# Placing side work in a one-core decoder step: value products, weight sums, load order, memory splits, convolution

## The chip, the cores and the metric

The kernel runs on one core of one Trainium2 chip. The metric is device time in microseconds of one execution. Before the change it is 1868.93 us, the median of 3 runs (1867.21 to 1870.87). The profile is of one execution.

The core has engines that run side by side, each with its own instruction queue: TensorE (PE, with its weight loads PEld), VectorE (DVE), ScalarE (ACT), GpSimd (POOL) and SyncE (SP), which here issues nearly all DMA transfers. An engine takes its instructions in the order in which the program was written out for it, and one that waits holds up all behind it.

## What is computed

One step of a one-layer hybrid decoder on 1024 prompt tokens and 8 x 4 sample tokens. Cut to what matters here:

```python
u, v, cq, ckv, kpe = split_in(rms_norm(xp, g_mix[l]) @ w_in[l])
a_out, _ = chunk_gmlp(u, v, w_s[l], b_s[l], ln_v_g[l], ln_v_b[l])
q = mla_queries(cq, pos_p, g_q_a[l], w_uq[l], g_qk_q[l])
k, vv = mla_keys_values(ckv_n, kpe, pos_p, w_uk[l], w_uv[l], g_qk_k[l])
b_out = mla_prompt_attend(q, k, vv)
xp = xp + merge_out(a_out, b_out, g_out_a[l], g_out_b[l], w_o[l])
mk, mv = mem_kv(mem_prompt, g_mem_in[l], w_mk[l], w_mv[l], g_mk[l])
xp = xp + mem_attend(rms_norm(xp, g_mem_x[l]), mk, mv, w_mq[l], g_mq[l], w_mo[l])
y, buf = conv_ffn(rms_norm(xp, g_ffn[l]), ..., w_up[l], w_conv[l], b_conv[l], w_down[l])
```

The sample tokens go through the same layer; their latent attention (`mla_sample_attend`) reads 8 x 4096 cached latents by a page table.

## The kernel before

Every large product is done in three matmuls: each float32 operand is split into a rounded part and a remainder (`split`, L187: the rounded part on ACT by default, the remainder on DVE), and `mm3` (L179) adds high x high, high x low and low x high. That is why almost all of PE's time stands under L185.

Tiles come from pools with a fixed number of buffers; a tile waits until the one that held its buffer before has been read for the last time. Where the program opens `manual_schedule` for an engine, that engine's instructions keep the order of the program text. Elsewhere a planner that models the engines' times sets the order.

*Phase 1* (`phase1`, L289) projects all tokens. For each half `hf` of the gated part it projects v (`proj`, L375), normalises it into `vgh`/`vgl` (L455 to L477), projects u (L485), and multiplies v by the gate matrices (L491 to L498). `squares` (L343) makes the inverse norms of the tokens; the engine of its root steps can be chosen. All v projections of the second half come in the next round of the loop.

*Phase 2a* (`phase2a`, L646) is the prompt's latent attention: 16 head units of 3 or 4 steps, 56 steps in all. PE, ACT, DVE and POOL follow the text. At each step `t` the loop (L763 to L794) runs the transposes, scores, exponentials and value products, and then everything listed in `extra[t]`. What stands in `extra` is set at L716 to L728: splits of the second half's weights (`split_w`), the sample tokens' projections (`tok_s`), the preparation of each head (`preps`: transposes of k and q, for head h of group 4 at steps 21 to 25), the projections of heads 4 to 7 (`late`, whose `norm` at L883 ends with the rope on POOL and with k at L906 and L907), and 26 `weight_sums` (L809). A weight sum loads 512 KB of weights on SP (L814 or L819), makes four additions on POOL (L822 to L825) and stores 512 KB on SP (L826). Its tile `wsum` has two buffers, which `split_w`'s raw weights use first. From step 32 on, `sample_prep` and `pages_ahead` (L1102) prepare the sample tokens: the latter loads the page numbers, the rope tables and the first three quads of latents.

*Phase 2b* (`phase2b`, L1119) is the sample tokens' attention: 128 pairs of page blocks, two to a quad of four pages, 16 to a request. `steps` (L1192) writes them out by hand for PE, ACT, DVE and POOL, from n = -10; SP is left to the planner. For a quad, POOL rotates the keys (`quad_rot`, L1307: `krq`), ACT and POOL or DVE split the latents (`quad_prep`, L1318: `ch`, `cl`), PE multiplies (`pair_score`, L1349), ACT squares (L1366, L1369), and PE forms the value products 20 pairs later (`quad_pv`, L1437). `quad_sums` (L1333) squares the rope keys of the second copy of the latents, `ck`. The ck pool has 15 buffers (L1132); the same buffers also serve `b4` (L1148), raw loads of phase 2a's last results, and at the end the raw weights and memory of the next stage (`raws`, L1204). At its start the text issues the load of `b4` (L1149), then inside `steps` those of `fold4` (L1201) and `wuv` (L1203).

*Behind it* come `mem_kv` (L1483: keys and values of the 256 memory tokens, with the last request's softmax and `batch_out` in between), `out_proj` (L1648), `mem_attention` (L1696) and `ffn` (L2070). In `ffn_up` (L2074) each of 11 rounds computes a `gate` block (L2115) for two halves h of the tokens, with the convolution behind it, and then two `value` blocks (L2160). `block` (L2086) makes seven products; `z` (L2098) is a DVE sum that frees one of two `X` buffers.

Of the kernel before, what the change touches and what calls it, by code (L numbers as in the profile page):

```python
# [6 lines left out]
FR = mybir.dt.float32r  # L7
I32 = mybir.dt.int32
AF = mybir.ActivationFunctionType
ALU = mybir.AluOpType  # L10
# [3 lines left out]
P = 128  # L14
# [140 lines left out]
class Net:  # L155
# [133 lines left out]
    def phase1(self):  # L289
# [140 lines left out]
        for hf in range(2):  # L430
# [8 lines left out]
            for i0, i1 in ((0, 3), (3, 6), (6, 8), (8, 9)):  # L439
                m, tn = i1 - i0, TILES[i0][1]  # L440
                if hf == 0 and i0 == 3:
                    squares(6, 8, nc.gpsimd)
# [203 lines left out]
    def phase2a(self):  # L646
# [69 lines left out]
        put(split_w, (2, 2, 3, 3))  # L716
        spread(tok_s, 0, 7)
# [9 lines left out]
        for j, x in enumerate(sums):  # L727
            extra[4 + j * 26 // 18 if j < 18 else 36 + (j - 18) * 13 // 8].append(lambda x=x: self.weight_sums(half(), *x))  # L728
# [390 lines left out]
    def phase2b(self):  # L1119
# [29 lines left out]
        nc.sync.dma_start(b4, self.b_dram)  # L1149
# [6 lines left out]
        for n in range(11):  # L1156
            at(n + 3 if n < 7 else 2 * n - 3, 0, lambda: next(mix, 0))
# [10 lines left out]
        at(last - 2, 3, lambda: self.split(*wk0, raws[0].rearrange("p (k n) -> p k n", k=8)))  # L1168
        for b in range(NB):
# [3 lines left out]
            for r, (k, pos) in enumerate(((12, 0), (13, 0), (14, 0), (14, 3), (15, 0), (16, 0), (17, 0), (17, 3), (18, 2), (19, 2), (20, 0), (20, 2), (21, 3))):  # L1173
# [8 lines left out]
                lambda b=b: self.batch_out(pt, st[b], 1, ppt),  # L1182
# [9 lines left out]
        def steps(n0, n1):  # L1192
            for n in range(n0, n1):
# [40 lines left out]
        with tc.manual_schedule(engines={E.SP}):  # L1234
# [5 lines left out]
            mem = self.mem_kv(raws, wk0)  # L1240
# [207 lines left out]
    def batch_out(self, p, s, part, pp=None):  # L1448
# [10 lines left out]
        nc.vector.tensor_scalar(oo[:, :256], oo[:, :256], rd, None, ALU.mult)  # L1459
# [23 lines left out]
    def mem_kv(self, raws, wk0):  # L1483
# [38 lines left out]
        def values(k):  # L1522
            wh, wl = (x.rearrange("p k n -> p (k n)").rearrange("p (k n) -> p k n", k=2) for x in self.stream(I["w_mv"][k // 2], 8))
            for i in range(2):
                t = slice(i * P, i * P + P)
                self.mm3(av[i], [(mh[:, k + e, t], ml[:, k + e, t]) for e in range(2)],
# [547 lines left out]
    def ffn_up(self, ops, rows, norm, first):  # L2074
# [40 lines left out]
        def gate(w, fs, h, prev):  # L2115
# [20 lines left out]
            nc.vector.tensor_tensor(G[:, :, 2:], G[:, :, 2:], row, ALU.mult)  # L2136
# [254 lines left out]
```

## Time and profile before

| | before |
|---|---|
| median of 3 runs | 1868.93 us |
| profiled execution, whole time | 1869.24 us |
| its span, first to last instruction | 1867.5 us |
| mean granted TensorE clock | 0.989 |

The page gives each engine's busy time, share of the span and number of instructions. A row of the list of waits names the waiting engine and line, the engine and line that ended the wait, and then total, count and longest wait in us. A row of the timeline gives start, duration, engine, line, operation, what it writes and reads, and in brackets the idle time ahead of it with its releaser. A row of the windows gives, for a stretch, the busy time of PE, PEld, DVE, ACT and POOL with their counts, the granted clock, and the DMA engines' busy share and GB/s. A row of DMA issues gives count, KB of one, and median us from issue to landing.

### The profile page before, as it was taken

The page shows a single profiled execution, that of the slowest core. Times are in us where ns is not written, and L with a number is a line of the kernel's source. Part 1 is how long each engine was busy: PE and PEld are TensorE (multiplying, and loading weights), DVE is VectorE, ACT ScalarE, POOL GpSimd, SP SyncE. Part 2 cuts the span into 40 slices and gives each one's busy share as a digit, 9 for nine tenths or more (in the row PEclk, how much of TensorE's full clock was granted, in tenths as well). Part 3 has the DMA queues.
Part 4 walks back from the last instruction along what each step waited for, and adds up shares of the span by engine and source line. Part 5 has one row for each costly group of instructions (what it writes and reads, how often), then busy time and mean ns, then how long its engine had stood idle before and what let it go on. Part 6 is the DMA issues. An engine that isn't in the chain of part 4 may idle for free.

```text
span 1867.5 us, 39356 instructions
## 1 busy us (share of the span) xinstructions
PE 1819.1 (97%) x14222; PEld 1713.6 (92%) x14222; DVE 1349.1 (72%) x2789; ACT 927.7 (50%) x1965; POOL 703.9 (38%) x862
## 2 busy tenths in 40 slices
PE   9999898998999999999999999999999999999999
PEld 8899776768999999998799978899999999999999
DVE  7864666665787667876645676889888898878664
ACT  7335676775555565555433456533323333344442
POOL 2011247524544444544223010267776677400000
PEclk9999899999999999999999999999999999999999
DMA  8101155547776666664554345312222222495252
GB/s 324 37 17 61 34 165 164 192 144 224 214 210 186 173 188 180 177 180 145 155 171 134 116 163 162 123 63 87 74 91 81 70 80 70 122 344 169 77 154 76
DMA packets 153187, 261.18 MB, mean 140 GB/s; under 512 B 20897, under 2 KB 97538, under 8 KB 152994
## 3 DMA queue, kind: packets, MB, share of 16 engines
q1 hardware_dynamic: 152130, 257.63, 44.7%
q8 instruction: 112, 1.84, 0.4%
q10 hardware_dynamic: 864, 1.05, 0.2%
q14 instruction: 81, 0.66, 0.1%
HBM read 212.79 MB, written 45.82 MB: 138 GB/s over the span
## 4 chain that ended last, share of the span: by engine, by line
PE 79%; issue 6%; DVE 5%; DMA 3%; SPq 3%; POOL 2%; ACT 2%; DVEq 0%; POOLq 0%; ACTq 0%
PE s L185 14%; PE d L185 12%; PE mm L185 9%; PE b L185 8%; PE X L185 7%; PE E L185 7%; PE F L185 7%; PE A L185 3%; PE y L185 2%; PE o L992 2%; PE tp L977 1%; PE tp L185 1%; SPq L1297 1%; PE o L1444 1%; DMA ck<-ck 1%
## 5 line engine op out<-in xcount | busy, mean ns | idle before, releaser
L185 PE MATMUL s<-w2h,ch 128*128 128x288 f32 (+1 forms) x1024 | 304.6, 297 | 0.0
L185 PE MATMUL s<-w2h,cl 128*128 128x288 f32 (+1 forms) x1024 | 296.9, 290 | 3.3 <-POOL cl L1329 3.3
L185 PE MATMUL s<-w2l,ch 128*128 128x288 f32 (+1 forms) x1024 | 295.6, 289 | 0.0
L185 PEld LDWEIGHTS s<-w2h,ch 128*128 128x128 f32 x1024 | 193.7, 189 | 8.3 <-issue 2.5
L185 PEld LDWEIGHTS s<-w2h,cl 128*128 128x128 f32 x1024 | 193.4, 189 | 5.5 <-POOL cl L1329 5.4
L185 PEld LDWEIGHTS s<-w2l,ch 128*128 128x128 f32 x1024 | 193.8, 189 | 0.0
L1372 DVE TENSOR_REDUCE ss<-sq 128x16 f32<-128x1024 f32 x128 | 155.3, 1213 | 32.5 <-ACT sq L1369 32.0
L1329 POOL TENSOR_TENSOR cl<-cT,ch 128x512 fp32r<-128x512 f32 x64 | 82.8, 1293 | 128.4 <-ACT ch L1325 115.9
L1369 ACT ACTIVATE sq<-s 128x512 f32<-128x512 f32 x128 | 76.5, 598 | 88.8 <-PE s L185 88.7
L1366 ACT ACTIVATE sq<-s 128x512 f32<-128x512 f32 x128 | 76.8, 600 | 74.7 <-PE s L185 74.3
L191 ACT CAST a<-brb 128x528 fp32r<-128x528 f32 x77 | 48.8, 634 | 112.5 <-PE d L185 105.8
L185 PE MATMUL d<-a,w 128*128 128x264 f32 x768 | 95.4, 284 | 1.1 <-DVE G L2168 1.1
L192 DVE TENSOR_TENSOR a<-brb,a 128x528 fp32r<-128x528 f32 x77 | 54.2, 706 | 57.6 <-ACT a L191 57.6
L185 PEld LDWEIGHTS d<-a,w 128*128 128x128 f32 x768 | 94.3, 188 | 1.3 <-issue 1.3
L2039 POOL TENSOR_TENSOR lo<-s,hi 128x1024 fp32r<-128x1024 f32 x20 | 63.1, 3154 | 45.7 <-ACT hi L2038 45.7
L185 PE MATMUL mm<-wlo,xh 128*128 128x256 f32 (+3 forms) x272 | 78.1, 289 | 0.1
L185 PE MATMUL mm<-whi,xh 128*128 128x256 f32 (+3 forms) x272 | 78.0, 288 | 0.0
L2094 ACT COPY a<-A 128x264 f32<-128x264 f32 x43 | 16.2, 376 | 124.5 <-PE A L185 116.3
L185 PE MATMUL mm<-whi,xl 128*128 128x256 f32 (+3 forms) x272 | 77.5, 289 | 0.0
L1325 ACT CAST ch<-cT 128x512 fp32r<-128x512 f32 x128 | 73.4, 626 | 2.6 <-PE tp L1005 2.6
L185 PE MATMUL d<-a,hi 128*128 128x264 f32 x552 | 72.0, 284 | 0.0
L1368 DVE TENSOR_TENSOR S<-s,S 128x64 f32<-128x64 f32 x128 | 28.0, 219 | 57.6 <-ACT sq L1366 57.3
(742 smaller groups left out, 6420.5 us busy)
## 6 DMA issues: line engine op xcount, KB each, us to landing
cT<-cT SPq DMA_DIRECT2D x256, 160.0 KB, 2.7
ck<-ck SPq DMA_DIRECT2D x256, 144.0 KB, 3.5
raw<-w_up SPq DMA_DIRECT2D x44, 512.0 KB, 3.6
wsumd<-wsum SPq DMA_DIRECT2D x26, 512.0 KB, 3.6
actd<-cv SPq DMA_DIRECT2D x44, 264.0 KB, 2.4
brb<-actd SPq DMA_DIRECT2D x44, 264.0 KB, 5.6
wsum<-w_down SPq DMA_DIRECT2D x22, 512.0 KB, 3.6
raw<-wsumd SPq DMA_DIRECT2D x20, 512.0 KB, 3.7
```

What stands on the lines that cost most here:

```text
L185: self.nc.tensor.matmul(out, l, r, start=first and i == 0, stop=last and i == len(seq) - 1)
L191: {"act": nc.scalar.copy, "pool": nc.gpsimd.tensor_copy, "dve": nc.vector.tensor_copy}[eng](hi, src)
L192: low = lambda: nc.vector.tensor_tensor(lo, src, hi, ALU.subtract)
L977: nc.tensor.transpose(tp[:, z * P : z * P + P], u[e][:, j * P : j * P + P], self.ident)
L992: nc.tensor.matmul(u["o"][g : g + 64, o : o + m * P], s["v"][:, j, h % 4], th[:, z * P : (z + m) * P], start=j == 0, stop=b == len(banks) - 1,
L1325: nc.scalar.copy(d["h"][:, k], src[k])
L1329: (nc.vector if k else nc.gpsimd).tensor_tensor(d["l"][:, k], src[k], d["h"][:, k], ALU.subtract)
L1366: nc.scalar.activation(sq[:, 0], ps[:, :, n0 : n0 + 256], AF.Square)
L1368: nc.vector.tensor_tensor(S, ps[:, :, sc : sc + 32], S, ALU.add)
L1369: nc.scalar.activation(sq[:, 1], pt.rearrange("p (e d) -> p e d", e=2), AF.Square)
L1372: yield lambda: nc.vector.tensor_reduce(s["ss"][:, g0 : g0 + 2].rearrange("p e (z h) -> p z e h", z=2), sq.rearrange("p z e (h d) -> p z e ...
L2039: eng.tensor_tensor(lo, src, hi, ALU.subtract)
```

## The change

Seven edits, in the order of the text:

1. `squares(6, 8)` makes its root steps on DVE instead of POOL; and in the first half the second half's first three v projections are written ahead of the gate products.
2. `split_w` moves from steps 2, 2, 3, 3 to 4, 5, 6, 7; `tok_s` from steps 0 to 7 to steps 4 to 11. The 26 weight sums move from steps 4 to 28 (18 of them) and 36 to 47 (8) to steps 7 to 11 (5), 25 to 31 (7) and 36 to 50 (14).
3. The loads of `b4`, `fold4` and `wuv` are each put, on SP, behind the page loads that the text has issued by then (n = 1, 16, 64). The steps of the mix that reads `b4` move from n = 3 to 15 to n = 5 to 17. `quad_sums` of the first quad moves from n = 1 to n = 4.
4. Four of the memory's eight splits move from `mem_kv` into the last steps of phase 2b, into two ck buffers.
5. The split of the first memory key weights moves from step 126 to 124.
6. The last request's normalisation runs on POOL instead of DVE.
7. `gate` becomes a generator that stops ahead of the convolution; in the first round both halves' products come first, then both convolutions. In the other rounds the order stays.

```diff
-                    squares(6, 8, nc.gpsimd)
+                    squares(6, 8)
...
+            if hf == 0:
+                ready.update({i: proj(w, i, 256) for i in range(3)})
             for g in range(4):
...
-        put(split_w, (2, 2, 3, 3))
-        spread(tok_s, 0, 7)
+        put(split_w, (4, 5, 6, 7))
+        spread(tok_s, 4, 11)
...
-        for j, x in enumerate(sums):
-            extra[4 + j * 26 // 18 if j < 18 else 36 + (j - 18) * 13 // 8].append(lambda x=x: self.weight_sums(half(), *x))
+        times = [*range(7, 12), *range(25, 32), *(36 + j * 16 // 14 for j in range(14))]
+        for t, x in zip(times, sums):
+            extra[t].append(lambda x=x: self.weight_sums(half(), *x))
...
-        nc.sync.dma_start(b4, self.b_dram)
...
-            at(n + 3 if n < 7 else 2 * n - 3, 0, lambda: next(mix, 0))
+            at((5, 6, 7, 8, 9, 10, 11, 12, 13, 15, 17)[n], 0, lambda: next(mix, 0))
...
-        at(last - 2, 3, lambda: self.split(*wk0, raws[0].rearrange("p (k n) -> p k n", k=8)))
+        at(last - 4, 3, lambda: self.split(*wk0, raws[0].rearrange("p (k n) -> p k n", k=8)))
+        mem0 = []
+
+        def mem_split(k):
+            if k % 2 == 0:
+                x = self.t(p, [P, 4, 288], FR, "ck", 15).rearrange("p k n -> p (k n)")[:, :1024].rearrange("p (k z n) -> p k z n", k=2, z=2)
+                mem0.extend((x[:, e, 0], x[:, e, 1]) for e in range(2))
+            self.split(*mem0[k], raws[1].rearrange("p (k n) -> p k n", k=4)[:, k], self.col("g_mem_in", k))
+
+        for k in range(4):
+            at(last - 3 + k, 3, mem_split, k)
...
-                if n == 16:
-                    nc.sync.dma_start(self.fold4, I["c_fold4"])
-                if n == 64:
-                    nc.sync.dma_start(wuv, I["w_uv"])
+                for k, dst, src in ((1, b4, self.b_dram), (16, self.fold4, I["c_fold4"]), (64, wuv, I["w_uv"])):
+                    if n == k:
+                        self.tc.add_manual_dep(
+                            nc.sync.dma_start(dst, src).ins, self.page_dma[-1].ins.name,
+                            mybir.DependencyInfo(mybir.DependencyClass.NoSync, mybir.DependencyReason.DATA), reason="order",
+                        )
...
-                    at(n + (6 if 0 <= Q < 2 else 3), 0, self.quad_sums, Q + 1, quads[Q + 1], st[(Q + 1) // 8])
+                    at(n + (6 if Q < 2 else 3), 0, self.quad_sums, Q + 1, quads[Q + 1], st[(Q + 1) // 8])
...
-        nc.vector.tensor_scalar(oo[:, :256], oo[:, :256], rd, None, ALU.mult)
+        if final:
+            nc.gpsimd.tensor_tensor(oo[:, :256], oo[:, :256], rd.broadcast_to([P, 256]), ALU.mult)
+        else:
+            nc.vector.tensor_scalar(oo[:, :256], oo[:, :256], rd, None, ALU.mult)
...
-        mh = self.t(p, [P, 8, 256], FR, "mh")
-        ml = self.t(p, [P, 8, 256], FR, "ml")
+        mh, ml = (self.t(p, [P, 4, 256], FR, x) for x in ("mh", "ml"))
...
-        xs = [(mh[:, k], ml[:, k]) for k in range(8)]
+        xs = mem0 + [(mh[:, k], ml[:, k]) for k in range(4)]
...
-                if h == 0:
-                    self.split(mh[:, k], ml[:, k], mr[k // 4][:, k % 4], self.col("g_mem_in", k))
+                if h == 0 and k > 3:
+                    self.split(*xs[k], mr[k // 4][:, k % 4], self.col("g_mem_in", k))
...
             nc.vector.tensor_tensor(G[:, :, 2:], G[:, :, 2:], row, ALU.mult)
+            yield G
...
-            return cv, G
+            yield cv
...
-            cvs, prev = [], None
+            cvs, prev, its = [], None, []
             for h in range(2):
-                cv, prev = gate(w, fs, h, prev)
-                cvs.append(cv)
+                it = gate(w, fs, h, prev)
+                prev = next(it)
+                its.append(it)
+                if q or h:
+                    cvs += [next(x) for x in its]
+                    its = []
```

More of the change, by code (lines that the diff above doesn't have):

```diff
@@ L1181, in phase2b @@
                 lambda b=b: self.batch_out(pt, st[b], 0),
-                lambda b=b: self.batch_out(pt, st[b], 1, ppt),
+                lambda b=b: self.batch_out(pt, st[b], 1, ppt, b == NB - 1),
                 lambda b=b: self.batch_close(pt, ppt, b, st.pop(b)),
@@ L1239, in phase2b @@
             self.wp = self.open("w", bufs=3, side="right")
-            mem = self.mem_kv(raws, wk0)
+            mem = self.mem_kv(raws, wk0, mem0)
             for f in late:
@@ L1446, in quad_pv, with batch_out @@
             )
-    def batch_out(self, p, s, part, pp=None):
+    def batch_out(self, p, s, part, pp=None, final=False):
         nc = self.nc
@@ L1481, in stream, with mem_kv @@
         return hi, lo
-    def mem_kv(self, raws, wk0):
+    def mem_kv(self, raws, wk0, mem0):
         nc, tc, I, O = self.nc, self.tc, self.I, self.O
@@ L1525, in values @@
                 t = slice(i * P, i * P + P)
-                self.mm3(av[i], [(mh[:, k + e, t], ml[:, k + e, t]) for e in range(2)],
+                self.mm3(av[i], [tuple(x[:, t] for x in xs[k + e]) for e in range(2)],
                          [(wh[:, e], wl[:, e]) for e in range(2)], first=k == 0, last=k == 6)
```

## The prediction

> **What bounds the kernel now.** I read the page first, then who TensorE (PE) waited for, then the granted clock around those waits.
>
> ```profile
> span 1867.5 us, 39356 instructions
> PE 1819.1 (97%) x14222; PEld 1713.6 (92%) x14222; DVE 1349.1 (72%) x2789; ACT 927.7 (50%) x1965; POOL 703.9 (38%) x862
> ```
>
> PE is busy 1819.1 of 1867.5 us. The change removes no matmul, so it can only win some of the 48 us in which PE stands still, and what those stops cost afterwards. The list of PE's waits (total, times, longest):
>
> ```profile
> PE tp L930 <- POOL k L907: 5.6, 2, 2.9
> PE tp L977 <- ACT pr L969: 5.2, 6, 1.3
> PE s L1344 <- ACT S L1347: 4.2, 1, 4.2
> PE mm L185 <- ACT vgh L191: 3.8, 1, 3.8
> PE m L1465 <- DVE oo L1459: 2.2, 1, 2.2
> PE X L185 <- DVE z L2098: 1.6, 1, 1.6
> PE b L185 <- DVE ml L198: 1.6, 2, 1.3
> PE b L185 <- ACT mh L195: 0.9, 1, 0.9
> ```
>
> Each edit aims at one of these rows. A stop also costs clock. Stretches just behind six of the stops, and one undisturbed stretch first (columns: busy time and count of PE, PEld, DVE, ACT, POOL, then the granted clock):
>
> ```profile
> 52.00:58.00 6.00, 6.00 (x53) 6.00 (x52) 5.92 (x27) 2.64 (x7) 0.00 (x0) 1.00 0.00 0
> 64.90:70.90 6.00, 6.00 (x24) 5.61 (x25) 4.52 (x18) 0.00 (x0) 0.00 (x0) 0.50 0.56 182
> 306.40:309.80 3.40, 3.40 (x13) 2.97 (x12) 3.02 (x8) 2.29 (x4) 3.16 (x5) 0.51 0.32 110
> 319.30:323.50 4.20, 4.20 (x20) 3.30 (x21) 0.00 (x0) 1.55 (x4) 3.89 (x6) 0.60 0.37 126
> 437.70:443.00 5.30, 5.30 (x23) 5.30 (x24) 3.52 (x5) 3.08 (x7) 3.03 (x4) 0.50 0.80 183
> 927.70:931.10 3.40, 3.40 (x13) 3.40 (x14) 2.02 (x5) 1.26 (x4) 0.00 (x0) 0.50 0.54 138
> 1207.60:1211.00 3.40, 3.40 (x18) 3.40 (x17) 3.37 (x4) 0.00 (x0) 3.40 (x2) 0.50 0.00 0
> ```
>
> PE counts as busy there but runs at half clock: 24 matmuls in 6 us against 53. A stop costs its idle time plus (1 - clock) times the slow stretch: 3.0, 1.7, 1.7, 2.7, 1.7 and 1.7 us in the order of the rows.
>
> The Trainium skill ("TensorE: Matmul & The Clock Gate", section "HAM oscillation — how this bites in real kernels") asks only that PE's gaps stay under about 3.4 us. The trace disagrees: half clock follows gaps of 2.2 and 1.6 us as well. By the page those two stops would cost 3.4 us less, and my sum would be smaller by that.
>
> **Part by part.** Times below are of the profiled execution.
>
> *Value products ahead of the gate's (L491), squares on DVE (L442).* PE stands 3.8 us before the first gate product, waiting for vgh. The change puts three projections of the next weight half there, 3 x 24 matmuls at 6.00/53 = 0.113 us, 8.1 us of work that is done later today anyway. They need only the split of v1; this cover is over twice the stall. If the cover failed the stall would stay as it is. Idle 3.8 + clock 3.0 = **-6.8 us**. Moving the small roots from POOL to DVE takes about 11 tiny instructions to DVE, where PE does not wait: 0.
>
> *Weight sums, splits and sample latents in phase 2a (L716 to L728).*
>
> ```profile
> 231.94 0.44 PE L977 MATMUL tp<-ident,pr 128*128 128x128 f32 x2 [1.31 <-ACT pr L969]
> 305.09 1.04 POOL L907 TENSOR_TENSOR k<-kr,hr 128x512 f32<-128x512 f32 x1
> 313.40 0.74 POOL L607 TENSOR_TENSOR rp<-q,tq_c 128x256 f32<-128x256 f32 x1
> 318.18 1.05 POOL L907 TENSOR_TENSOR k<-kr,hr 128x512 f32<-128x512 f32 x1
> 311.22 0.49 DVE L894 TENSOR_TENSOR rq<-hr,sq_tok 128x16 f32<-128x16 f32 x1
> L822 POOL TENSOR_TENSOR wsum<-wsum 128x256 f32<-128x256 f32 x13 | 9.5, 728 | 23.4 <-DMA wsum<-w_down 23.4
> 391.05 0.74 POOL L825 TENSOR_TENSOR wsum<-wsum 128x256 f32<-128x256 f32 x1
> 417.57 0.13 POOL L1269 MEMSET S<- 128x32 f32 x1 [25.78 <-PE tp L977]
> 419.89 0.46 POOL L1314 TENSOR_TENSOR krq<-cT,cosT 128x128 f32<-128x128 f32 x1 [2.19 <-PE o L992]
> 422.62 0.46 PE L1344 MATMUL s<-bd,krq 128*128 128x128 f32 x2 [0.23 <-DVE b_last L1009]
> wsum<-w_down SPq DMA_DIRECT2D x7, 512.0 KB, 3.5
> wsumd<-wsum SPq DMA_DIRECT2D x7, 512.0 KB, 3.3
> SPq L814 <- DMA wsumd<-wsum: 73.6, 22, 4.7
> ```
>
> Today POOL's rope for heads 4 to 7 stands behind weight sums, and PE waits for k twice (5.6 us idle, 3.4 us clock). With no sums in steps 12 to 24 both go but for about 1 us: -8. The splits and latents leave ACT's path in steps 0 to 3, where waits for pr lie (the 1.3 us at 231.9 is the longest of the six); I take -3, that one and its slow clock of 1.7 (bounds 0 and -5.2, all six). So PE would reach the end of phase 2a about 11 us earlier.
>
> But POOL runs in program order, and phase 2b opens with POOL's krq, for which its first PE instruction waits. The sums have two buffers, and each load waits for the store before it (the wait of L814). One buffer's round is load 3.5, four subtractions of 0.73 with their gaps 3.2, store 3.3: 10.0 us, so 5.0 us a sum at best. Measured, the 13 sums between 319.2 and 391.8 took 72.6/13 = 5.6 us each. Before, POOL is then free for 25.8 us. After, only five sums are done before step 25 and 21 come behind it. They can start when the second k is done: its input at 311.2, less 4.5 (first stall and its clock) and 3, plus 5.8 of rope (313.40 to 319.23) = 309.5. 21 x 5.6 end at **427**, against krq at 419.9 today and PE done near 411. Bounds: 21 x 5.0 ends at 414; the SP queue's page work moves the other end:
>
> ```profile
> 384.98 0.40 SPq L1107 DMA_DIRECT2D pages<-pages  x1
> 391.62 9.03 SPq L1297 DMA_DIRECT2D cT<-cT  x12
> ```
>
> From the page numbers to the last latent SP is held 15.7 us. Where that falls among the sums it delays them by up to 10: 437. With 1.6 for krq (its three instructions) PE starts phase 2b at 428.6 instead of 422.6: **+6** (-7 to +16). The gains inside phase 2a are swallowed by this seam; PE idles some 18 us ahead of it. I add **+2.7** of clock behind that stop, the row of 437.70 being the nearest (bounds 1.7 and 3.0).
>
> *First latents ahead of constants (L1149, L1200 to L1213).*
>
> ```profile
> 428.60 0.33 SPq L1149 DMA_DIRECT2D ck<-b  x1
> 429.12 1.87 SPq L1301 DMA_DIRECT2D ck<-ck  x4
> 436.11 0.31 ACT L1337 ACTIVATE ksq<-ck 128x128 f32<-128x128 f32 x1 [8.25 <-DMA ck<-ck]
> ```
>
> ACT stands 8.25 us for the first ck quad, whose load is issued behind the constants; behind it on ACT are the squares and S, for which PE waits 4.2 us. After, that load goes first and its square comes three pairs later. Even if SP reaches it only after the last sum's store, three pairs (over 9 us) cover the 7 us from issue to 436.1. Idle 4.2 + clock 2.7 = **-6.9**. The b load now waits behind pages, but the mix reads it from pair 5 on: 0.
>
> *Memory splits (L1171, L1503).*
>
> ```profile
> 867.14 0.84 SPq L1207 DMA_DIRECT2D ck<-memT  x2
> 879.83 1.94 PE L1444 MATMUL o<-ck,S 128*32 128x257 f32 x32
> ```
>
> Four of eight splits move ahead of the end of the pairs, which would remove the 2.5 us of the mh and ml rows. But their results take two slots of the 15 ck slots. Today both halves of memT load at 867.1; with one slot taken between them, the second half must wait for the value products at 879.8 to 881.8. At 3.5 us like the other 512 KB loads it lands at 885, and PE has used up the four finished steps (12 matmuls at 0.113, 1.4 us) by 883.2. I take **+1** (-2.5 to +3.5).
>
> *Last normalisation on POOL (L1456).*
>
> ```profile
> 923.67 0.16 DVE L1458 RECIPROCAL rd<-m 128x1 f32<-128x1 f32 x1
> 927.13 0.35 DVE L1459 TENSOR_SCALAR oo<-oo,rd 128x256 f32<-128x256 f32 x1
> ```
>
> On DVE it is queued behind a split whose load is late. POOL is free; its 128x256 product costs 0.73 (row L822), so oo is ready near 924.6 instead of 927.5, before PE gets there. 2.2 + 1.7 = **-3.9**.
>
> *Convolution of the first block behind both gates (L2180).*
>
> ```profile
> 1202.29 2.48 DVE L2145 SCALAR_TENSOR_TENSOR cv<-G,cols,cv 128x528 f32<-128x528 f32 x2
> ```
>
> z waits on DVE behind this convolution. It now runs later, under value products; DVE has the same work until then. 1.6 + 1.7 = **-3.3** (0 if DVE, which is nearly full here, only passes the delay on).
>
> **Sum**: -6.8 + 6 + 2.7 - 6.9 + 1 - 3.9 - 3.3 = -11.2 us. The profiled execution took 1869.24 us, within 0.3 us of the median 1868.93, so the median becomes 1857.7, rounded to 1858.
>
> **Rivals.**
>
> *The seam is not bound by POOL.* Then PE starts phase 2b at 411.6, 11 us early, and no clock is lost there: -6.8 - 11 - 6.9 + 1 - 7.2 = -30.9, 1838 us. For it: 25.8 us of idle POOL today. Against: eight sums more behind the second k, at 5.0 at least, are 40 us. Chance 0.17.
>
> *The sums come so late that the kernel gets slower.* One mechanism: SP's page work stands behind or among the last sums, and krq waits for both. The rest wins 17.2 us without the seam (6.8 + 6.9 + 3.9 + 3.3 less 1 and 2.7), so it decides from a start of phase 2b 17 us later than 422.6, at 440. If the sums run at 5.9, a little above the measured 5.6, and the whole 15.7 us is added, krq comes at 309.5 + 124 + 15.7 = 449 and PE at 451: +28 - 17.2, 1880 us; the middle of such cases is 1873. For it: both bounds exist in the rows. Against: the hold of SP overlaps waits that the sums have anyway. Chance 0.15.
>
> *The wins hold but the seam eats nearly all of them*, PE starting between 436 and 443: 1869 us, no change. Chance 0.08.
>
> **How the numbers follow.** My forecast, with PE starting phase 2b between 416 and 436 (1844 to 1866 us), has 0.60. The range takes in the first rival's 1838 at its edge and reaches into the slower case: 1838 to 1871. About 0.2% (3.7 us) is what a measurement can tell from no change: faster 0.60 + 0.17 = 0.77, same 0.08, slower 0.15.
>
> **What would show it.** Right: no PE wait for vgh, for POOL k (or one under 1.5 us), for S L1347, for oo or for z; a new PE stop of 10 to 25 us ahead of the first L1344, put down to POOL krq or the latents, with POOL busy on weight sums until about 420 (7 us earlier on the clock of the whole span, since phase 1 ends sooner). Wrong: POOL idle ahead of the first krq (then the time is nearer 1838), or a stop above 30 us there (then it is slower). The memory step is wrong if PE waits less than 1 us for mh and ml.

## The result, and the profile after

The changed kernel takes 1877.82 us (median of 20 runs, 1874.17 to 1884.29) against 1869.95 us before (median of 20, 1865.32 to 1872.97). The ratio is 1.0043, 95% interval 1.0035 to 1.0052: slower by 0.43%, where 1858 us was forecast, in a range of 1838 to 1871. The profiled execution took 1874.82 us, 1873.1 of it span. That is 3 us under the median, so the table of stages below accounts for 5.6 of the 7.9 us between the two medians.

The head of the page after:

```profile
span 1873.1 us, 39347 instructions
PE 1816.2 (97%) x14222; PEld 1710.1 (91%) x14222; DVE 1347.5 (72%) x2796; ACT 927.7 (50%) x1965; POOL 693.9 (37%) x850
```

PE stands still for 1873.1 - 1816.2 = 56.9 us instead of 48.4, with the same 14222 matmuls. The list of PE's waits after (total, times, longest) says where:

```profile
PE s L1358 <- POOL krq L1330: 10.1, 1, 10.1
PE tp L980 <- ACT pr L972: 6.0, 8, 1.1
PE tp L980 <- ACT cn L1049: 5.6, 1, 5.6
PE b L185 <- DVE ck L198: 5.4, 2, 4.0
...
PE m L1270 <- ACT olT L1483: 3.0, 1, 3.0
...
PE X L185 <- DVE z L2114: 1.6, 1, 1.6
```

The rows of before for vgh, for POOL k, for ACT S and for oo are gone, as the edits meant. In their place stand krq, cn, ck and olT, of which the prediction had the first alone. To see what each stage won or lost, I took the start of its first PE instruction from both traces (us; the last column is the prediction's terms for that stage):

| stretch | before | after | change | predicted |
|---|---|---|---|---|
| start to first score product of 2a | 206.37 | 199.93 | -6.4 | -6.8 |
| phase 2a, to the first product of 2b | 216.25 | 228.01 | **+11.8** | +6 |
| 2b, first to sixth quad | 36.35 | 30.98 | -5.4 | -6.9 + 2.7 |
| sixth quad to first memory product | 423.70 | 424.69 | +1.0 | 0 |
| first memory product to m<-wuv | 50.77 | 54.05 | **+3.3** | +1 - 3.9 |
| m<-wuv to last y | 247.70 | 250.46 | **+2.8** | 0 |
| last y to product 150 of A | 120.01 | 118.58 | -1.4 | -3.3 |
| the rest | 566.37 | 566.41 | 0 | 0 |

They add to +5.6 us of span, against -11.2. Phase 2a and the memory stage are the largest misses, by 5.8 and 6.2 us; what follows the memory stage misses by 2.8 more.

**Phase 2a.** PE did get ahead, as predicted. The same transpose of the sample's latents, before and then after:

```profile
354.61 0.38 PE L1045 MATMUL tp<-ident,cns 128*32 128x128 f32 x2
335.04 0.38 PE L1048 MATMUL tp<-ident,cns 128*32 128x128 f32 x2
```

Counted from the first score product of each (206.37 and 199.93), PE was 13.1 us ahead there, where 11 was forecast for the end of the phase. It lost all of that again. Rows of POOL's timeline after (start, duration, engine, line, operation; in brackets the idle time before it):

```profile
295.76 1.05 POOL L910 TENSOR_TENSOR k<-kr,hr 128x512 f32<-128x512 f32 x1 [5.62 <-ACT pth L982]
296.76 0.73 POOL L825 TENSOR_TENSOR wsum<-wsum 128x256 f32<-128x256 f32 x1
...
310.45 0.73 POOL L828 TENSOR_TENSOR wsum<-wsum 128x256 f32<-128x256 f32 x1
321.91 0.45 POOL L609 TENSOR_TENSOR rp<-qs,tq_c 32x128 f32<-32x128 f32 x1 [10.73 <-ACT kTh L191]
...
341.55 0.72 POOL L828 TENSOR_TENSOR wsum<-wsum 128x256 f32<-128x256 f32 x1
342.21 0.41 POOL L1039 MEMSET bdq<- 128x64 f32 x4
342.55 0.31 POOL L1040 MEMSET cn<- 128x258 f32 x1
...
396.65 0.73 POOL L825 TENSOR_TENSOR wsum<-wsum 128x256 f32<-128x256 f32 x1 [9.50 <-DMA wsum<-w_down]
...
425.74 0.72 POOL L828 TENSOR_TENSOR wsum<-wsum 128x256 f32<-128x256 f32 x1
427.43 0.46 POOL L1330 TENSOR_TENSOR krq<-krq,krq 128x128 f32<-128x128 f32 x1
```

As predicted, 21 sums run between the second k and krq. But they are no unbroken chain. Three run up to 311.2, then POOL waits 10.73 us to rope the sample's queries (L609), which stands ahead of the other 18 in POOL's order. Those 18 take from 323.4 (three short products after that row) to 426.5: 5.7 us each, the forecast's 5.6 with the 9.50 us of SP's page work in it. Had the 21 run on from the second k (done at 296.8) at 5.6 us, the last would have ended at 414.4; it ended 12 us later, and PE's stop for krq is 10.1 us. So the hole accounts for the whole stop, by this sum; no run moves the rope alone.

The same order does a second thing. The rows of ACT and PE at that place, and PE's first of phase 2b:

```profile
342.90 0.36 ACT L1049 COPY cn<-tp 32x256 f32<-32x256 f32 x1 [6.98 <-POOL cn L1040]
343.31 0.90 PE L980 MATMUL tp<-ident,pr 128*128 128x128 f32 x3 [5.63 <-ACT cn L1049]
427.94 0.58 PE L1358 MATMUL s<-bd,krq 128*128 128x128 f32 x1 [10.11 <-POOL krq L1330]
```

The zeroing of cn, 0.31 us long, waits on POOL behind the sums of steps 25 to 31; ACT waits 6.98 us for it and PE 5.63 us for ACT. The granted clock behind these stops and behind two of the memory stage (columns as in the prediction's table of stretches; the number after the engines is the clock):

```profile
343.40:361.40 18.00, 17.73 (x69) 13.40 (x70) 8.48 (x32) 9.07 (x28) 10.02 (x14) 0.50 0.62 199
428.00:433.20 5.20, 5.20 (x21) 4.89 (x22) 2.12 (x3) 2.00 (x5) 5.04 (x8) 0.50 0.88 249
887.70:893.90 6.20, 3.13 (x14) 3.13 (x15) 5.94 (x10) 3.99 (x6) 5.20 (x7) 0.50 0.15 58
938.50:941.70 3.20, 3.20 (x24) 3.03 (x23) 0.56 (x2) 1.84 (x4) 0.00 (x0) 0.50 0.23 68
```

Behind cn the clock stays at half for 18 us, although PE counts as busy for 17.73 of them. The Trainium skill ("TensorE: Matmul & The Clock Gate", section "What's actually happening") has full clock come back after one busy window of about 3.4 us; taken by the profile's busy time, this row disagrees, and the measurement decides. Behind krq it is 5.2 us, half of it lost, 2.6: the forecast's 2.7.

**Memory stage.** Timeline rows after, of DVE, POOL, PE and ACT:

```profile
880.92 1.87 DVE L198 SCALAR_TENSOR_TENSOR ck<-ck,cols,ck 128x256 fp32r<-128x256 f32 x1
...
885.60 0.48 DVE L198 SCALAR_TENSOR_TENSOR ck<-ck,cols,ck 128x256 fp32r<-128x256 f32 x1
...
887.12 2.64 DVE L198 SCALAR_TENSOR_TENSOR ml<-ck,cols,mh 128x256 fp32r<-128x256 f32 x4
889.68 0.18 DVE L222 TENSOR_SCALAR rqx<-ss 128x64 f32<-128x64 f32 x1
...
890.24 0.48 DVE L198 SCALAR_TENSOR_TENSOR ck<-ck,cols,ck 128x256 fp32r<-128x256 f32 x1
...
880.95 1.56 POOL L1404 TENSOR_TENSOR S<-S,ss 128x768 f32<-128x768 f32 x1 [1.01 <-DVE ss L236]
...
887.29 0.47 POOL L1397 TENSOR_TENSOR ss<-ss,kss 128x64 f32<-128x64 f32 x1 [4.73 <-DVE ss L1386]
...
886.13 0.39 PE L185 MATMUL b<-ck,wk0h 128*128 128x256 f32 x1 [1.42 <-DVE ck L198]
...
890.77 0.58 PE L185 MATMUL b<-ck,wk0h 128*128 128x256 f32 x1 [4.02 <-DVE ck L198]
...
936.61 0.91 ACT L195 ACTIVATE mx2h<-raw,cols 128x256 fp32r<-128x256 f32 x2 [1.56 <-DMA raw<-mix]
937.42 0.19 ACT L1483 COPY olT<-m 128x64 f32<-128x64 f32 x1
937.67 0.52 PE L1270 MATMUL m<-wuv,olT 128*32 128x64 f32 x6 [2.96 <-ACT olT L1483]
```

The fourth split's remainder (890.24) stands on DVE behind the four remainders of `mem_kv`'s own splits (887.12, 2.64 us together) and the root of the last request (L222), whose input POOL makes at 887.29. DVE has no gap there. And where oo no longer stops PE, the next instruction does: olT stands on ACT behind mx2h, which waits for a DMA. And the remainder of the second split (880.92) took 1.87 us beside a POOL product of 1.56, where the third (885.60) took 0.48 us with POOL idle. The Trainium skill ("GPSIMD Engine Reference", section "8. Key points") says that the two engines share interfaces when a DVE instruction has two SBUF inputs; the rows agree.

### The profile page after: what moved, and what is told of

Same layout as the page of the kernel before. It is cut to its first block, busy times and chain, and to the rows that moved or that the text cites. A ratio compares the mean times of both kernels' runs of the same rounds, so it can differ in the third digit from the quotient of the medians.

```text
span 1873.1 us, 39347 instructions
## 1 busy us (share of the span) xinstructions
PE 1816.2 (97%) x14222; PEld 1710.1 (91%) x14222; DVE 1347.5 (72%) x2796; ACT 927.7 (50%) x1965; POOL 693.9 (37%) x850
## 4 chain that ended last, share of the span: by engine, by line
PE 76%; issue 6%; DMA 5%; SPq 4%; DVE 4%; POOL 3%; ACT 1%; DVEq 0%; POOLq 0%; ACTq 0%
PE s L185 12%; PE d L185 12%; PE mm L185 9%; PE b L185 7%; PE F L185 7%; PE X L185 7%; PE E L185 7%; PE A L185 3%; PE y L185 3%; SPq L1311 2%; SPq L1315 2%; PE o L995 1%; PE tp L185 1%; PE tp L980 1%; DMA wsumd<-wsum 1%
## 5 line engine op out<-in xcount | busy, mean ns | idle before, releaser
L185 PE MATMUL s<-w2h,cl 128*128 128x288 f32 (+1 forms) x1024 | 296.8, 290 | 3.3 <-POOL cl L1343 3.3
```

Source lines behind the costliest of these rows:

```text
L185: self.nc.tensor.matmul(out, l, r, start=first and i == 0, stop=last and i == len(seq) - 1)
```

## Experiments

Each ratio is against the kernel before on the same chip, with its 95% interval. r1 to r4 share a chip, and so do r5 to r8, r9 to r12, r13 to r16, and r17 with r18.

**r1_sums_back: the weight sums at their old steps.**

```diff
-        times = [*range(7, 12), *range(25, 32), *(36 + j * 16 // 14 for j in range(14))]
-        for t, x in zip(times, sums):
-            extra[t].append(lambda x=x: self.weight_sums(half(), *x))
+        for j, x in enumerate(sums):
+            extra[4 + j * 26 // 18 if j < 18 else 36 + (j - 18) * 13 // 8].append(lambda x=x: self.weight_sums(half(), *x))
```

> The 26 weight sums at their old steps, all else as in the changed kernel. Theory (the late sums hold POOL, and with it the end of phase 2a): the stop for cn near 337 us and most of the 10.1 us stop for krq go, the two stops for k come back; 10 to 16 us faster than the changed kernel, so 2 to 8 us faster than before. Rival (the seam is late for the loads of pages and latents, whatever POOL does): the krq stop stays above 7 us and the time is within 4 us of the changed kernel.

Measured: 1872.91 us, 1.0018 (1.0008 to 1.0028). The krq and cn stops are gone, and the wait for k is back, 12.7 us where before had 5.6:

```profile
PE tp L932 <- POOL k L909: 12.7, 2, 9.6
```

Some 5 us are won back by undoing the placing, so it did cost; but 10 to 16 were expected, and the time is still above that of before. The old steps don't do well beside the later weight splits of this edit either. Those hold the two buffers until step 7: the first sum starts 43.4 us into phase 2a instead of 35.4, and the ropes of heads 4 to 7, which stand behind the sums, come later.

**r2_cn_dve: the zeroing of cn on VectorE.**

```diff
-        nc.gpsimd.memset(self.cn, 0.0)
+        nc.vector.memset(self.cn, 0.0)
```

> The zeroing of cn runs on DVE instead of POOL, so ACT no longer waits for it behind weight sums; all else as in the changed kernel. Theory (the chain of sums on POOL sets when phase 2b starts): the 5.6 us stop and the slow clock behind it go, but the krq stop grows by nearly as much, 0 to 4 us faster. Rival (the cn stop with its 20 us at half clock is the loss itself): 10 to 14 us faster.

Measured: 1876.61 us, 1.0035 (1.0022 to 1.0048). Of the list of PE's waits:

```profile
PE s L1358 <- POOL krq L1330: 15.2, 1, 15.2
...
PE tp L980 <- ACT bdq L1061: 4.8, 1, 4.8
```

The memsets of bdq, in front of cn on POOL, take its place, and phase 2a is no shorter (228.92 us against 228.01). The stop for krq is 5.1 us longer. So PE reaches the end of 2a earlier and waits for krq longer: the cn stop, for all its 18 us of half clock, costs nearly nothing as long as POOL's chain sets the time of the seam.

**r7_three_buffers: a third buffer for the sums** (and five buffers instead of six for the transposed probabilities, for room).

```diff
-        half = lambda: self.t(pm, [P, 2, 2, 256], F32, "wsum", 2)
+        half = lambda: self.t(pm, [P, 2, 2, 256], F32, "wsum", 3)
...
-            th = u["t", b] = self.t(p, [P, 512], F32, "pth", 6)
+            th = u["t", b] = self.t(p, [P, 512], F32, "pth", 5)
```

> The changed kernel with three buffers for the weight sums instead of two, and five buffers instead of six for the transposed probabilities (to make room). Theory (the round of one buffer, load 3.5 + subtractions 3.2 + store 3.3 us, sets 5 to 5.6 us a sum): a sum takes 3.5 to 4 us, the chain of 21 ends 20 us or more earlier, the POOL krq stop is under 2 us, the cn stop is at most as long as it was, and the time is 1862 to 1870 us. Rival (SP's order or the DMA engines themselves set the pace, not the buffers): the krq stop stays at 8 us or more and the time is 1873 us or more. If the five buffers for the probabilities cost something, it shows as a new PE or ACT wait for pth in the attention stage.

Measured: 1866.16 us, 0.9988 (0.9975 to 1.0000), 11.7 us under the changed kernel. POOL's rows at both ends of the 18 sums:

```profile
323.68 0.72 POOL L825 TENSOR_TENSOR wsum<-wsum 128x256 f32<-128x256 f32 x1
...
408.79 0.73 POOL L828 TENSOR_TENSOR wsum<-wsum 128x256 f32<-128x256 f32 x1
409.54 0.46 POOL L1328 TENSOR_TENSOR krq<-cT,cosT 128x128 f32<-128x128 f32 x1
```

The 18 sums now take 85.8 / 18 = 4.8 us each instead of 5.7. That is more than the 3.5 to 4 expected, in part since SP's page work still stands among them (one wait of 8.7 us for a load). Phase 2a is 16.5 us shorter (211.55). The round of two buffers thus sets the pace. The hole ahead of the rope is still there, 14.66 us long, yet PE waits for krq only 1.3 us: krq is late where hole and pace come together.

**r4_first_only: the kernel before, with the value products and the squares of the first edit alone.**

```diff
-                    squares(6, 8, nc.gpsimd)
+                    squares(6, 8)
...
+            if hf == 0:
+                ready.update({i: proj(w, i, 256) for i in range(3)})
```

> The kernel before with the first edit alone (root steps on DVE, three value projections ahead of the gate products). Theory: the 3.8 us stop and its slow clock go and nothing gives it back, 5 to 8 us faster than before. Rival (a later stage takes it back): within 2 us of before.

Measured: 1863.41 us, 0.9967 (0.9954 to 0.9981). The first stretch is 200.17 us, 6.2 shorter. This edit does what was predicted, and by itself it beats both kernels.

**r3_mem_back: the changed kernel with the memory splits as before.**

```diff
-        at(last - 4, 3, lambda: self.split(*wk0, raws[0].rearrange("p (k n) -> p k n", k=8)))
+        at(last - 2, 3, lambda: self.split(*wk0, raws[0].rearrange("p (k n) -> p k n", k=8)))
...
-        for k in range(4):
-            at(last - 3 + k, 3, mem_split, k)
```

> The four memory splits and the split of the first key weights back at their old places, all else as in the changed kernel. Theory (the fourth split's remainder stands on DVE behind the last request's root, which waits for POOL): the PE waits for DVE ck L198 (5.4 us) go, those for mh and ml (2.5 us) come back, 3 to 6 us faster. Rival (the loss there comes from the rest of the seam, whatever the splits do): within 1.5 us.

Measured: 1872.7 us, 1.0009 (0.9995 to 1.0023). The memory stage takes 50.25 us again, against 54.05, 3.8 less; the median is 5.1 us under the changed kernel's. The stops for ck are gone, as the theory said.

**r5_no_2a_no_mem: the changed kernel with the whole of the 2a edit and the memory edit undone** (r1, r3 and):

```diff
-        put(split_w, (4, 5, 6, 7))
-        spread(tok_s, 4, 11)
+        put(split_w, (2, 2, 3, 3))
+        spread(tok_s, 0, 7)
```

> The changed kernel with the placing of the phase-2a work (weight sums, splits, sample latents) and the memory splits as before: the value products, the latents ahead of the constants, the last normalisation and the convolution order stay. Theory (the losses lie in the weight sums and the memory splits alone): the stops ahead of the first L1358 and at ACT cn are gone, the two POOL k stops are back at 5 to 6 us, 2b starts 9 us earlier than before (as with the value products alone), the sixth quad 14 to 16 us earlier, and the end 14 to 18 us earlier: 1851 to 1856 us, ratio 0.990 to 0.993. Rival (the latents ahead of constants win locally only, and the clock or the DMA queue takes it back later): the end is no earlier than with the value products alone, 1861 to 1866 us, ratio 0.995 to 0.998.

Measured: 1862.09 us, 0.9956 (0.9940 to 0.9972): the rival's range. The first edit and the three others together are worth no more than the first alone. For the latents, SP's waits around the start of 2b say why; before first, then r5:

```profile
SPq L1201 <- DMA b<-b_all: 3.7, 1, 3.7
...
SPq L1149 <- DMA mix<-q: 0.3, 1, 0.3
```

```profile
SPq L1305 <- DMA mix<-q: 5.0, 1, 5.0
```

The first ck load cannot go before the store of mix has landed, whichever order SP has. Before, the constants were issued in the shadow of that wait; now SP waits 5.0 us with nothing to issue. The load goes out 6.2 us after PE's first product of 2b instead of 6.5.

**r6_placed: r5 with the sums at other steps**, ten ahead of the late ropes, six ahead of the sample's memsets, ten behind them.

```diff
+        times = [4, 5, 6, 7, 8, 9, 10, 11, 12, 13, 24, 25, 26, 27, 27, 28, *(34 + j for j in range(10))]
+        for t, x in zip(times, sums):
+            extra[t].append(lambda x=x: self.weight_sums(half(), *x))
```

> As r5_no_2a_no_mem, but with the weight sums at steps 4 to 13 (ten, ahead of the late ropes), 24 to 28 (six) and 34 to 43 (ten). Theory (the sums are one chain of some 5.6 us a sum on POOL, and their price is set by which POOL work stands behind them): with ten done early instead of five, the chain ends some 28 us earlier than in the changed kernel, so no POOL krq stop; with none between steps 14 and 23 the POOL k stops are under 2 us; with none in steps 29 to 33 the cn stop is under 2 us. 2b starts 13 to 18 us earlier than before and the time is 1843 to 1850 us. Rival (the old spread, with its 5.6 us of k stops, is as good as this chain allows): a new POOL stop of 5 us or more appears (k, cn or krq), and the time is within 3 us of r5_no_2a_no_mem.

Measured: 1853.83 us, 0.9919 (0.9904 to 0.9934), 8.3 us under r5 on the same chip and the lowest median of the study. No stop for k, cn or krq ahead of 2b is left, and POOL is idle ahead of its first work there:

```profile
391.59 0.73 POOL L828 TENSOR_TENSOR wsum<-wsum 128x256 f32<-128x256 f32 x1
405.35 0.12 POOL L1274 MEMSET S<- 128x32 f32 x1 [13.04 <-ACT pth L982]
```

The expectation of 1843 to 1850 us counted from r5 at 1851 to 1856; the difference of the two, 6 to 8 us for the placing itself, was right.

**r12_r6_no_latents, r13_one_three_placed, r14_one_placed, r16_sums_only: what the latents ahead of the constants are worth.** r12 is r6 with this edit undone; r13 is r6 without the normalisation and the convolution; r14 is r13 with the latents undone, so before plus the first edit and the new steps of r6; r16 is r14 with the second half of the edit alone:

```diff
-                    at(n + (6 if 0 <= Q < 2 else 3), 0, self.quad_sums, Q + 1, quads[Q + 1], st[(Q + 1) // 8])
+                    at(n + (6 if Q < 2 else 3), 0, self.quad_sums, Q + 1, quads[Q + 1], st[(Q + 1) // 8])
```

> r6_placed with the latents' loads behind the constants and the first two quads' sums as before. Theory (the first ck load waits for the mix<-q store to land, not for the constants, so the new order brings the load only some 1 us forward, and the wait for S is replaced by one for S and krq behind late cT loads): PE waits some 4 us for ACT S again, the first to the sixth quad take 35.5 to 36.5 us instead of 34.1, and the time is 1 to 4 us above r6_placed, 1854 to 1858 us. Rival (the prediction's step, 6.9 us): 1859 to 1862 us.

> The kernel before with the value products ahead, the latents ahead of the constants and the weight sums as in r6_placed; memory splits, last normalisation and convolution as before. Theory (the normalisation and the convolution order are worth next to nothing): within 3 us of r6_placed, 1851 to 1857 us, with a wait for oo of 0.5 to 2.3 us and for z of 1.6 us. Rival (the two are worth 7 us together, as predicted): 1859 to 1862 us.

> r13_one_three_placed with the latents' loads and first sums as before. Theory (the edit is worth about 2 us where phase 2b starts early): 1 to 3 us above r13_one_three_placed, the stop for ACT S back at 4 us, first to sixth quad 1.5 to 2.5 us longer than there. Rival (the prediction's 6.9 us): 5 to 8 us above it.

> r14_one_placed with the sums of the first quads three pairs later, the loads in their old order. Theory (the wait for S goes because the squares of the first ck quad no longer stand ahead of S on ACT, whatever the load order): no stop for ACT S of 1 us or more, in its place one of 1 to 3 us for POOL S or krq, and first to sixth quad within 1 us of r13_one_three_placed. Rival (the load order is what removes it): the stop for ACT S stays at 3 us or more.

Measured: r12 1859.14 us, 0.9953 (0.9938 to 0.9968); r13 1857.71 us, 0.9932 (0.9914 to 0.9950); r14 1856.49 us, 0.9937 (0.9918 to 0.9957); r16 1861.07 us, 0.9949 (0.9930 to 0.9969). r12, 5.3 us above r6 on another chip, is in the rival's range, though in the stretch that the edit touches it loses only 1.8 us (35.92 against 34.09); its profile also has a phase 2a 4.3 us longer, with the same placing. On one chip r13 and r14 are the same within their intervals: the latents' edit, with its predicted 6.9 us, is worth nothing that can be told. Their stretches from the first to the sixth quad are 33.90 and 34.76 us. r16's waits beside r14's row say what the halves do; r14 first:

```profile
PE s L1348 <- ACT S L1351: 3.5, 1, 3.5
```

```profile
PE s L1348 <- POOL S L1273: 2.3, 1, 2.3
PE s L1348 <- POOL krq L1320: 2.1, 2, 1.4
```

The later sums alone remove the wait for ACT S, with the loads in their old order. What comes in its place is a wait for POOL's zeroing of S, which stands behind a krq whose own latents are late, and r16's stretch is no shorter (36.16 us): a miss for the half of the expectation that said it would be within 1 us of r13's.

**r8_r5_no_norm and r9_r5_no_conv: r5 with the normalisation back on VectorE, and with the convolution back in its place.**

```diff
-                lambda b=b: self.batch_out(pt, st[b], 1, ppt, b == NB - 1),
+                lambda b=b: self.batch_out(pt, st[b], 1, ppt),
```

```diff
-                if q or h:
+                if True:
                     cvs += [next(x) for x in its]
```

> As r5_no_2a_no_mem, with the last normalisation back on VectorE. Theory (the wait for ACT olT stands behind the same DMA, so the normalisation on POOL wins next to nothing): PE waits for DVE oo again by 1.5 to 3 us instead of ACT olT, and the time is within 2 us of r5_no_2a_no_mem. Rival (the prediction's step: 3.9 us): the time is 3 to 5 us above r5_no_2a_no_mem.

> As r5_no_2a_no_mem, with the convolution of the first block back in its old place. Theory (the convolution's new order wins at most 1 to 1.5 us, since PE waits 1.6 to 1.7 us for DVE z either way): the wait for z is still 1.6 us, the stretch from the last y product to product 150 of A is 0.8 to 1.5 us longer than in r5_no_2a_no_mem (118.6 us there), and the time is within 3 us of it. Rival (the prediction's step: 3.3 us): 3 to 4 us more.

Measured: r8 1860.08 us, 0.9958 (0.9943 to 0.9973); r9 1861.94 us, 0.9964 (0.9952 to 0.9975); r5 is 1862.09. Neither edit is worth anything that can be told. r5's wait in the place of oo, and then the two of r8:

```profile
PE m L1260 <- ACT olT L1473: 3.3, 1, 3.3
```

```profile
PE m L1260 <- ACT olT L1473: 1.4, 1, 1.4
...
PE m L1472 <- DVE oo L1466: 0.7, 1, 0.7
```

With the normalisation on POOL PE arrives earlier at the same late olT. For the convolution even the small win expected was too much: from the last y to product 150 of A takes 118.57 us in r9 and 118.58 in r5. The 1.4 us by which the changed kernel was ahead of the kernel before there is not the edit's. PE stops 1.6 to 1.7 us for z in 17 of the 20 profiles, with the edit and without; in before alone half clock follows, for 3.4 us, which costs 1.7. (r13 lacks both and is 3.9 us above r6, on another chip and with overlapping intervals; r5, r8 and r9 show none of that.)

**r10_split_earlier and r11_placed_split: the fourth memory split beside the third**, in the changed kernel and over r6's placing.

```diff
-            at(last - 3 + k, 3, mem_split, k)
+            at(last - 3 + min(k, 2), 3, mem_split, k)
```

> The changed kernel with the fourth memory split one pair earlier, beside the third. Theory (the 4.0 us stop in the memory stage is the fourth split's remainder standing on VectorE behind the last request's root, which waits for POOL): the 4.0 us stop for ck L198 is gone, its stretch of half clock is shorter or gone, and from the first memory product to m<-wuv it takes 46 to 50 us instead of 54.05 in the changed kernel and 50.76 before; the time is 1870 to 1875 us. Rival (the ck slots and the late memT load cause it): the stop stays at 3 us or more, and the time stays at 1874 to 1881 us.

> r6_placed with the change's memory splits, the fourth beside the third: the whole change, with the weight sums, weight splits and sample latents placed anew and one split moved. Theory: the memory stage (first memory product to m<-wuv) takes 1 to 4 us less than in r6_placed (49.3 us), so the time is 1849 to 1854 us, ratio 0.989 to 0.992. Rival (what the splits win is taken by the late w_mk load or ACT olT behind it): the stage is as long as in r6_placed or longer, and the time 1853 to 1858 us.

Measured: r10 1876.05 us, 1.0044 (1.0030 to 1.0058); r11 1861.37 us, 0.9956 (0.9940 to 0.9972). In r10 the 4.0 us stop is gone, as the theory said, but the stage still takes 53.52 us instead of 46 to 50, and the time is in the range of the rival: what is lost there was not lost to that stop. In r11 it takes 56.65 us, 7.3 more than in r6. Its stretches (columns as above):

```profile
868.30:873.30 5.00, 2.69 (x21) 2.26 (x18) 5.00 (x10) 2.26 (x7) 0.97 (x2) 1.00 0.98 380
873.30:883.50 10.20, 9.06 (x38) 7.95 (x38) 6.25 (x8) 5.25 (x10) 8.51 (x14) 0.50 0.23 69
```

In the first 5 us DVE is busy without a gap and PE for half of the time, and then 10.2 us run at half clock.

**r15_storage_only, r17_splits_wk_late, r18_storage_wk_late: which part of the memory edit costs it.** r15 is r11 with the four results in their new slots, but the splits in their old place; r18 is r15, and r17 is r11, with the split of the weights wk0 back at its old step.

```diff
-            self.split(*mem0[k], raws[1].rearrange("p (k n) -> p k n", k=4)[:, k], self.col("g_mem_in", k))
...
-                if h == 0 and k > 3:
+                if h == 0:
```

```diff
-        at(last - 4, 3, lambda: self.split(*wk0, raws[0].rearrange("p (k n) -> p k n", k=8)))
+        at(last - 2, 3, lambda: self.split(*wk0, raws[0].rearrange("p (k n) -> p k n", k=8)))
```

> r11_placed_split with the first four splits' results in the ck slots as there, but the splits themselves done in their old place, when the memory products begin. Theory A (VectorE is full from the last pairs to the last request's root, and splits put there delay that root and themselves): without them there the memory stage is as long as in r6_placed (49.3 us) within 1 us, and the time is 1852 to 1857 us. Theory B (the slots that the results take delay the second half of memT and w_mk): PE waits for ACT mh or the split of the second half by 2 us or more, the stage takes 52 to 57 us, the time is 1858 to 1863 us.

> r11_placed_split with the split of wk0 back in its old place, two pairs later. Theory (that split, waiting for ScalarE on VectorE, makes the root of the last requests 2.4 us late): the waiting remainder of wk0 no longer stands ahead of the root's steps, the memory stage is 2.5 us or more shorter than in r11_placed_split (56.65 us), at 50 to 54 us, and the time is 1855 to 1859 us. Rival (the moved memory splits themselves): the stage stays at 55 us or more, the time at 1859 to 1864 us.

> r15_storage_only with the split of wk0 back in its old place: of the memory edit only the storage is left. Theory (the early split of wk0 made the stage of r15_storage_only 53.8 us long): the stage is 49 to 51 us and the time 1851 to 1856 us. Rival (the ck slots, with the later second half of memT and w_mk): the stage stays at 52.5 us or more, the time at 1857 to 1861 us.

Measured: r15 1859.1 us, 0.9946 (0.9927 to 0.9966), stage 53.77 us; r18 1857.5 us, 0.9948 (0.9935 to 0.9961), stage 51.63; r17 1863.69 us, 0.9965 (0.9951 to 0.9979), stage 56.80. By its length and time r15 is in the range of theory B. r18's stage lies between its two theories, its time in the rival's range. From r6's 49.30 us the new slots add 2.3 (r18), the earlier split of wk0 another 2.1 (r15), the earlier splits 2.9 more (r11). These are single profiles, and where this edit is undone the stage takes 49.1 to 50.8 us, so the steps are good to some 1.5 us each, their sum of 7.3 well clear of that. Without the earlier wk0 the splits alone add 5.2 (r17 over r18), so the theory of r17 falls. One piece of it is the prediction's own mechanism; in r17's timeline ACT waits for the second half of memT:

```profile
876.97 1.71 ACT L195 ACTIVATE mh<-ck,cols 128x256 fp32r<-128x256 f32 x4 [3.06 <-DMA ck<-memT]
```

None of the three parts wins. How the loss divides among DVE's order, the late loads and the clock is not settled.

## Why the prediction was wrong, step by step

- **Value products ahead of the gate's: right.** -6.8 predicted, -6.4 after and -6.2 alone.
- **Weight sums, splits and sample latents: the step that failed most.** That krq would wait for a chain of 21 sums was right, as were 5.6 us a sum (5.7 measured) and the 2.7 us of clock. Wrong was to let all 21 run on from the second k without a break, 21 times 5.6 us, to 427: the order written for POOL puts the sample's rope (L609) between the third and the fourth of them, and POOL waits 10.73 us there. Phase 2a grew by 11.8 us, not 6. It was luck that the miss is only 5.8: the hole makes the end of the chain 12 us late, but the second k was done 96.9 us into phase 2a, 6.3 earlier than the prediction's 309.5. The same order delays the memsets of bdq and cn, which no step of the prediction looked at; r2 shows that this stop is hidden behind the other. The 3 us taken for the waits for pr did not come as idle time, which is 6.0 us in 8 waits instead of 5.2 in 6; over the first 93.6 us of the phase the granted clock was 0.98 instead of 0.93, but in r4, which does not move them, it was 0.96.
- **First latents ahead of constants: right in the trace of the changed kernel, wrong in its reason.** The prediction had the load "issued behind the constants". It waits for the store of mix to land (5.0 us in r5), and the constants filled that wait. The stretch is 5.4 us shorter in the changed kernel because phase 2b started late: the store had landed, and the load went out 0.8 us ahead of PE's first product. With a prompt start the edit wins 0.9 to 1.8 us in its stretch (r13 and r14, r6 and r12), and r13 and r14 take the same time: of the term of -6.9 nothing can be told.
- **Memory splits: a cost that was sized too small.** +1 was taken, with bounds of -2.5 and +3.5 us; the stage grew by 3.3 in the changed kernel and by 7.3 over r6. The stops for mh and ml went, and stops of 5.4 us for ck came. The slots named are about a third of the 7.3 (2.3, r18). What was left out is at least in part the work of DVE, which has no gap at the start of that stage (5.00 of 5.00 us in r11).
- **Last normalisation on POOL and convolution behind both gates: a stall moved, not removed.** The terms of -3.9 and -3.3 took a stop's idle time as its price, and did not ask what is late next. It is olT behind a DMA in the one place. In the other it is z itself: in the changed kernel z (1215.79) still stands on DVE behind the convolution, which now begins at 1209.22, and PE waits 1.6 us for it as before. The prediction's own bound of 0 was the answer there. Its 1.7 us of clock behind that stop was a trait of one execution.

Against the sum of -11.2, phase 2a missed by 5.8 us, the memory stage by 6.2, the stretch behind it by 2.8, the convolution by 1.9 and the pairs by 1.0, the value products by 0.4; phase 2b's start did 1.2 better. Together that is the 16.8 us between -11.2 and +5.6, but for rounding. The 2.8 us are in part the stop's clock: before, the half clock behind oo lies ahead of m<-wuv; after, it lies behind it (938.5 to 941.7). Of the rivals, the slower one came nearest: its middle of 1873 us and its case of 1880 lie on either side of the time. But its mechanism, page work among the last sums, gave only the 9.50 us which the bounds had; the rest is the hole ahead of the rope. The other rival, a seam not bound by POOL, is what r6 makes true by another placing; it gave 1853.83 us, not 1838, since phase 2a won 6.3 us of the 11, and the latents and the last two edits did not add what that sum counted.

## What to carry to other kernels

Before a chain of work on an in-order engine is priced by its rate, write down every foreign instruction between its links, and what each of them waits for; then price the small instructions that now stand behind the chain. A stop on the list of waits is worth its length only if the next arrival behind it is early: look up what that engine waits for next, and from which DMA. And a load is as early as the last transfer that it must wait for (here the store of mix), not as early as its place in the queue.

## What the runs showed of the hardware

- The half clock outlasts a stop by very different times: 3.2 us behind olT, 5.2 us of running behind krq, 18 us behind cn, in one execution.
- The placing of r6 in phase 2a is the same in r11 to r18, and its length falls into two groups: 208.1 to 209.9 us (r6, r11, r14, r15, r18) and 214.0 to 214.2 us (r12, r13, r16, r17). In both groups PE stops twice for DVE pr, near 300 and near 320 to 326 us: by 0.5 to 1.4 us in the shorter ones, by 1.2 to 2.3 in the longer, and only the longer have half clock there, for 6.8 us in all. So one profile can be 4 us off in this stage alone, and a difference of that size between two profiles is no evidence.
- The remainder of a 128x256 split on DVE took 1.87 us beside a POOL product of 1.56 us, and 0.48 alone.
